# Hybrid decoder layer on one core: the last layer norm placed behind the first up weights, a ring shared by U and the down-weight sums, and row tiles used as the up projection's wide tiles

## The chip, the cores and the metric

The kernel runs on one core of one Trainium2 chip. The metric is the device time of one execution in microseconds, lower is better. All inputs and the output are float32.

## The reference, cut to what matters

One layer is computed on 2048 tokens of width 1024, with 16 learned tokens put ahead of them. An input projection feeds three mixers (a short convolution, a gated linear recurrence and a pooling group), whose outputs go through one output projection. Then:

```python
x = layer_norm(ALPHA * x + mix, ln1_g, ln1_b)
u = causal_dwconv(x @ w_up, w_ffn_conv, b_ffn_conv)     # w_up: 1024 x 5632, three taps over tokens
gate, val = jnp.split(u, 2, axis=-1)
ffn = (jax.nn.silu(gate) * val) @ w_down                # w_down: 2816 x 1024
out = layer_norm(ALPHA * x + ffn, ln2_g, ln2_b)
```

## The kernel before, in words

**Precision.** Each float32 operand is split into a high part (ScalarE cast, line 109) and a low part (VectorE difference, line 110), and each product is three TensorE matmuls: high by high, high by low, low by high.

**Mixers** (class Mixers, 0 to about 956 us). The tokens go in four blocks of 512 (b = 0 to 3). `out_proj` (lines 583 to 603) multiplies by w_o in two halves of columns, adds the residual to row tiles of 128 x 1024 (line 596), normalizes the rows (`layer_norm`, `norm_rows`, lines 188 to 208: bn_stats 199, square root on ScalarE 202, two fused VectorE passes 205 and 207) and stores them to x1 in DRAM (line 603). Of the last block this is done by `run_last`. `columns` (line 643) later reads x1, transposes it on TensorE (line 667) and writes x1T. Row tiles come from the pool `rows`, a ring of six.

**Up projection** (class Ffn, about 956 to 1940 us). x @ w_up is computed in two halves of 1024 tokens (b = 0, 1) by a Winograd form of Strassen's scheme: of the four blocks of x and of w_up, sums are made, and seven products stand for eight. A pair (`up_pair`, lines 895 to 963) is one tile of 128 gate columns and one of 128 value columns; there are 22 pairs per half. Its products, in this order, are a11 x b11, s2 x t2, a12 x b21, s1 x t1, s3 x t3, s4 x b22, a22 x t4 (`product`, line 892): 7 x 4 x 3 matmuls, 168 in half 0 (two column groups each) and 84 in half 1. ScalarE copies the first result to a tile U (line 921), and VectorE adds the others onto U, cg and cv (926, 935, 940, 944, 948). cg and cv also take two halo columns from GpSimd (905, 906). Then come the convolution (956, 959), silu (961) and the product yv (962). Before the change U, cg, cv and yg have one tile each and yv three. Every two pairs (ya and yb) give four sums on GpSimd into a tile a_t (975 to 978) and seven stores to a_ops (982); there is one tile a_t, used by `prepare` and `fetch` too.

- Weights: `load_pair` (829) loads them; in half 0 the weight sums s1 to s4 are made on GpSimd (846 to 849) and stored to s_up (852, 853), in half 1 they are loaded back (841, 842). `weights` (871) splits them. For the very first pair `begin` (864) loads and splits early: a11 and a12 lie in two row tiles.
- x operands: `prepare(0)` makes those of half 0. `prepare(1)` (740) makes those of half 1 on the side, in four steps: four piece loads from x1T (737), four GpSimd sums (751 to 754) into a_t, seven stores to x_ops (760). `fetch` and `take` (763 to 795) read all seven operands back during the last pair of half 0 and split them into the place of the old ones, each once its product has been done: first operand into a_t, the others through the ring `piece` of four tiles of 128 x 512.
- Down-weight sums: `down_sums` (987 to 1005) runs on the side of half 1 in 44 steps, each with two loads (996) into a piece, four GpSimd instructions (1000 to 1003) and one store (1004).

**Down projection** (`down`, from about 1940 us): seven products again, layer norm, output.

**What orders the work.** TensorE runs in program order. On every other engine and DMA queue a scheduler at build time fixes the order: among the instructions whose inputs and buffer slots are free by its own reckoning it takes the one earliest in the program. `high_priority(offset=AHEAD)` moves weights 1000 instructions ahead, and `layer_norm` is moved 300 back (BEHIND). Slots of a ring are given out as they come free. `weave` (1091) places two steps of the side work after each pair. On the chip each queue then runs strictly in its order. Loads and stores of the up stage go through SyncE's queue (SP).

## Time and profile before

| | us |
|---|---|
| median of 3 runs | 2404.72 (2399.98 to 2404.72) |
| profiled execution | 2401.31 |
| its span | 2399.6 |
| TensorE busy | 2262.4 (94%) |
| VectorE busy | 1678.5 (70%) |
| ScalarE busy | 890.0 (37%) |
| GpSimd busy | 852.0 (36%) |

Engines in the profile: PE is TensorE's matmuls, PEld its weight loads, DVE is VectorE, ACT ScalarE, POOL GpSimd, SP SyncE, and SPq, ACTq, POOLq are their queues. Times in rows are us from the span's start and durations in us, unless a row is a summary with "min/median/max" or "mean ns". "[x <-Y]" means that the engine sat idle for x us before the instruction and that Y ended the wait. PEclk is the granted TensorE clock as a share of full speed. An "xN" counts instructions.

### The profile page before, as it was taken

Reading aid. Unit: us, or ns where it says so; the run is one execution under the profiler, and the core shown is the slowest. Engines: PE = TensorE matmul, PEld = TensorE weight load, DVE = VectorE, ACT = ScalarE, POOL = GpSimd, SP = SyncE. Lnnn points to the kernel's source line nnn. Section 1 sums busy time; section 2 is a strip of 40 time slices with the busy share of each in tenths; the row PEclk is TensorE's granted clock in tenths of the full one; section 3 lists DMA queues with packets and bytes.
Section 4 is the critical chain, followed back from the end, with each engine's and each line's share of the span. In section 5 each row is a group of like instructions: output and inputs, shape, how many; then the busy total and the mean of one; then the engine's idle time right before and its main releaser. Section 6 shows DMA issues by size and latency. Waiting matters only on the chain.

```text
span 2399.6 us, 34046 instructions
## 1 busy us (share of the span) xinstructions
PE 2262.4 (94%) x12692; PEld 1930.7 (80%) x12692; DVE 1678.5 (70%) x2277; ACT 890.0 (37%) x1400; POOL 852.0 (36%) x870
## 2 busy tenths in 40 slices
PE   8999999999999998899979998877899999999996
PEld 6898777788888886799979997666788887887785
DVE  4676868687867878777767788655677766476658
ACT  3234322422342244344423445323344454334332
POOL 3451523152423344344465445677311113000300
PEclk9999999999999999899989999988999999999998
DMA  5212223322632264455675447677544476567553
GB/s 205 71 63 98 71 71 117 126 79 80 200 121 80 79 196 167 159 192 176 221 237 185 152 155 230 197 210 212 178 140 146 141 259 226 185 207 274 179 192 132
DMA packets 183737, 384.36 MB, mean 160 GB/s; under 512 B 17026, under 2 KB 78674, under 8 KB 183444
## 3 DMA queue, kind: packets, MB, share of 16 engines
q1 hardware_dynamic: 168180, 339.81, 43.0%
q10 hardware_dynamic: 14496, 40.06, 4.6%
q0 software_dynamic: 896, 2.33, 0.4%
q8 instruction: 99, 1.62, 0.3%
q14 instruction: 66, 0.54, 0.1%
HBM read 274.58 MB, written 107.55 MB: 159 GB/s over the span
## 4 chain that ended last, share of the span: by engine, by line
PE 69%; POOL 8%; DVE 8%; DMA 6%; issue 6%; ACT 2%; SPq 1%; POOLq 0%; DVEq 0%; ACTq 0%
PE bank L892 25%; PE bank L1035 13%; PE bank L114 9%; PE bank L116 8%; PE bank L115 8%; PE bank L397 3%; DVE w_lo L110 3%; DMA piece<-in_w_down_dram 1%; DMA row<-x 1%; POOL piece L1001 1%; POOL piece L1002 1%; POOL piece L1000 1%; DVE row L205 1%; DVE row L207 1%; DMA piece<-x_ops 1%
## 5 line engine op out<-in xcount | busy, mean ns | idle before, releaser
L110 DVE TENSOR_TENSOR w_lo<-raw,w_hi 128x512 fp32r<-128x512 f32 (+1 forms) x467 | 481.5, 1048 | 288.2 <-ACT w_hi L109 278.3
L109 ACT CAST w_hi<-raw 128x512 fp32r<-128x512 f32 (+1 forms) x467 | 359.3, 787 | 785.6 <-PE bank L116 261.2
L1035 PE MATMUL bank<-w_hi,w_lo 128*128 128x512 f32 x616 | 241.9, 393 | 10.2 <-DVE w_lo L110 10.2
L1035 PE MATMUL bank<-w_hi 128*128 128x512 f32 x616 | 240.4, 390 | 3.6 <-ACT w_hi L109 3.6
L1035 PE MATMUL bank<-w_lo,w_hi 128*128 128x512 f32 x616 | 240.4, 390 | 0.0
L114 PE MATMUL bank<-xhi,w_hi 128*128 128x512 f32 (+1 forms) x640 | 234.3, 366 | 0.0
L109 ACT CAST w_hi<-s 128x1024 fp32r<-128x1024 f32 x88 | 92.1, 1048 | 379.6 <-PE bank L892 248.3
L110 DVE TENSOR_TENSOR w_lo<-s,w_hi 128x1024 fp32r<-128x1024 f32 x88 | 125.8, 1430 | 144.2 <-ACT w_hi L109 144.2
L116 PE MATMUL bank<-xhi,w_lo 128*128 128x512 f32 (+1 forms) x640 | 225.1, 352 | 0.1
L115 PE MATMUL bank<-xlo,w_hi 128*128 128x512 f32 (+1 forms) x640 | 224.4, 351 | 0.0
L1035 PEld LDWEIGHTS bank<-w_hi,w_lo 128*128 128x128 f32 x616 | 116.0, 188 | 39.6 <-DVE w_lo L110 16.0
L1035 PEld LDWEIGHTS bank<-w_hi 128*128 128x128 f32 x616 | 116.0, 188 | 27.7 <-ACT w_hi L109 4.1
L1035 PEld LDWEIGHTS bank<-w_lo,w_hi 128*128 128x128 f32 x616 | 115.9, 188 | 25.1
L1068 POOL TENSOR_TENSOR row<-row,du 128x512 f32<-128x512 f32 x24 | 47.6, 2015 | 248.3 <-DVE du L1066 246.5
L116 PEld LDWEIGHTS bank<-xhi,w_lo 128*128 128x128 f32 x640 | 120.2, 188 | 17.3 <-DVE w_lo L110 0.5
L114 PEld LDWEIGHTS bank<-xhi,w_hi 128*128 128x128 f32 x640 | 120.5, 188 | 16.4 <-ACT chi L109 0.5
L115 PEld LDWEIGHTS bank<-xlo,w_hi 128*128 128x128 f32 x640 | 120.7, 189 | 15.0 <-issue 0.7
L959 DVE SCALAR_TENSOR_TENSOR yv<-cv,f_taps,yv 128x1024 f32<-128x1024 f32 x88 | 120.9, 1374 | 9.8 <-POOL cv L906 3.1
L892 PE MATMUL bank<-xb22h,w_hi 128*128 128x258 f32 (+2 forms) x264 | 77.5, 348 | 50.1 <-DVE cv L935 50.1
L959 DVE SCALAR_TENSOR_TENSOR yg<-cg,f_taps,yg 128x1024 f32<-128x1024 f32 x88 | 120.2, 1366 | 2.9 <-POOL cg L905 1.0
L114 PE MATMUL bank<-w_hi,xhi 128*128 128x512 f32 x272 | 112.9, 415 | 7.8 <-ACT xhi L109 7.8
L423 POOL TENSOR_TENSOR work<-work,pre 128x256 f32<-128x256 f32 (+1 forms) x96 | 89.0, 927 | 83.7 <-DVE pre L426 60.8
(291 smaller groups left out, 5766.0 us busy)
## 6 DMA issues: line engine op xcount, KB each, us to landing
raw<-a_ops SPq DMA_DIRECT2D x70, 512.0 KB, 4.7
raw<-in_w_up_dram SPq DMA_DIRECT2D x66, 512.0 KB, 4.6
raw<-in_w_feat_dram SPq DMA_DIRECT2D x64, 512.0 KB, 3.3
s_up<-s SPq DMA_DIRECT2D x44, 512.0 KB, 2.7
a_ops<-a_t SPq DMA_DIRECT2D x88, 256.0 KB, 2.0
s<-s_up SPq DMA_DIRECT2D x44, 512.0 KB, 4.6
raw<-s_down SPq DMA_DIRECT2D x40, 512.0 KB, 3.6
a_ops<-yv SPq DMA_DIRECT2D x66, 256.0 KB, 2.4
```

The costliest lines, as they stand in the source:

```text
L109: self.nc.scalar.copy(hi, src)
L110: self.nc.vector.tensor_sub(lo, src, hi.bitcast(F32))
L114: mm(out, lhsT=a_hi, rhs=b_hi, start=first, stop=False)
L115: mm(out, lhsT=a_hi, rhs=b_lo, start=False, stop=False)
L116: mm(out, lhsT=a_lo, rhs=b_hi, start=False, stop=last)
L205: nc.vector.scalar_tensor_tensor(r[:n], in0=r[:n], scalar=mv[:n, t, 0:1], in1=self.g_sb[:n], op0=ALU.subtract, op1=ALU.mult)
L397: mm(pt[:, t * P:(t + 1) * P], lhsT=ka[:, c:c + P], rhs=qa[:, c:c + P], start=True, stop=True)
L423: self.key_eng.tensor_mul(postv[:, :, 0, :], postv[:, :, 0, :], prev[:, :, 1, w - 1:w].to_broadcast(end))
L892: mm(u[:, 0:n], lhsT=wp[:, kc], rhs=xp[o][k][:, at:at + n], start=start, stop=k == 3 and i == 2, skip_group_check=True)
L959: nc.vector.scalar_tensor_tensor(y, in0=c[:, d:UT + d], scalar=self.taps[:, i, d:d + 1], in1=y, op0=ALU.mult, op1=ALU.add)
L1035: mm(bank, lhsT=x, rhs=y, start=first and k == 0 and i == 0, stop=k == HK - 1 and i == 2, skip_group_check=True)
L1068: nc.gpsimd.tensor_add(rows[t][:, f], rows[t][:, f], us[u])
```

## The change

The pool `rows` is opened on the other side of memory and stays open through the up projection; cg, cv, yg and yv of every pair are taken from its six tiles. The layer norm and the x1 stores of the last block of tokens become `end_block`, called after the split of the first pair's weights instead of at the end of `out_proj`; gain and shift are loaded a second time for it, into the tile a_t. `prepare(1)` stores only the four sums, with one DMA per step, and `fetch` reads b11, b21 and b22 from x1T. `take` becomes a generator: four of its seven operands are taken during the last pair of half 0 (after the first three products and at the end) and three during the first pair of half 1. In half 1, U is a tile of the ring `piece` (four tiles, now 514 wide), which the down-weight sums use at that time. The stores of the up weight sums are written into the program at the start of their own pair instead of the next one. The constants of the up stage are released together with it.

```diff
 def open_out(self, ctx):
...
-        self.rows = ctx.enter_context(self.tc.tile_pool(name="rows", bufs=6, side="right"))
...
+    def open_rows(self, ctx):
+        self.rows = ctx.enter_context(self.tc.tile_pool(name="rows", bufs=6, reuse_waits="tile"))
...
-    def load_norm(self, pool, g, b):
-        self.g_sb = pool.tile([P, D], F32, tag="ln_g", name="ln_g")
+    def norm_tiles(self, pool):
+        return [pool.tile([P, D], F32, tag=f"ln_{i}", name=f"ln_{i}") for i in "gb"]
+    def load_norm(self, tiles, g, b):
+        self.g_sb, self.b_sb = tiles
...
 def out_proj(self, b, half, res):
...
-        if half == 1:
-            cm.layer_norm(res[:TT], P)
...
+        if half == 1 and b + 1 < NB:
+            self.end_block(b, res)
+
+    def end_block(self, b, res):
+        cm, nc, tiles = self.cm, self.nc, self.row_tiles(b)
+        cm.layer_norm(res[:TT], P)
+        if b == 0:
+            cm.layer_norm(res[TT:], NM)
+        for (c, n), r in zip(tiles, res):
+            (nc.scalar if b + 1 < NB else nc.sync).dma_start(self.x1[b * TB + c:b * TB + c + n, :], r[0:n])
...
 class Ffn, __init__:
-        self.x_dram = [None] + [dpool.tile([7, P, 4 * UT // 2], F32, name=f"x_ops{b}") for b in range(1, UB)]
+        self.x_dram = [None] + [dpool.tile([4, P, 4 * UT // 2], F32, name=f"x_sums{b}") for b in range(1, UB)]
...
 def prepare(self, b):
...
+                if b:
+                    nc.sync.dma_start(self.x_dram[b][:, :, k * w:(k + 1) * w].rearrange("i p c -> p i c"), t)
+                    continue
...
-                for i, o in enumerate(X_OPS):
-                    if b == 0:
-                        cm.split(self.x_hi[o][k][:, at:at + w], self.x_lo[o][k][:, at:at + w], ops[o])
-                    else:
-                        nc.sync.dma_start(self.x_dram[b][i, :, k * w:(k + 1) * w], ops[o])
+                for o in X_OPS:
+                    cm.split(self.x_hi[o][k][:, at:at + w], self.x_lo[o][k][:, at:at + w], ops[o])
...
 def fetch(self, b):
...
+        def source(o, k):
+            if o[0] == "t":
+                return self.x_dram[b][int(o[1]) - 1, :, k * h:(k + 1) * h]
+            c = 2 + b * UT + (int(o[2]) - 1) * h
+            return self.cm.x1T[(int(o[1]) - 1) * 4 + k, :, c:c + h]
...
+        whole = self.a_tile()
+        for o in X_OPS:
             for k in range(4):
-                raw = self.piece()
-                self.nc.sync.dma_start(raw, self.x_dram[b][i, :, k * h:(k + 1) * h])
+                raw = whole[:, k, :] if o == X_OPS[0] else self.piece()
+                self.nc.sync.dma_start(raw, source(o, k))
                 yield o, k, raw
...
 def take(self, b):
...
-        def done(o):
+        while ready:
             for _ in range(4):
...
+            yield
...
-    def y_tile(self, name):
-        return self.ypool.tile([P, UT + 2], F32, tag="yv", name=name, bufs=3)
...
-    def piece(self):
-        return self.ypool.tile([P, UT // 2], F32, tag="piece", name="piece", bufs=4)
+    def piece(self, name="piece", n=UT // 2):
+        return self.ypool.tile([P, XW], F32, tag="piece", name=name, bufs=4)[:, 0:n]
...
 def load_pair(self, b, j):
...
-        self.store_sums()
-        self.store_sums = lambda: None
...
+    def store_sums(self, j, sums):
+        for i, s in enumerate(sums):
+            self.nc.sync.dma_start(self.s_up[j, :, i * 1024:(i + 1) * 1024], s)
...
 def up_pair(self, b, j, begun=None, done=lambda: None):
...
-        w = self.weights(*(begun or self.load_pair(b, j)))
-        U = self.upool.tile([P, XW], F32, tag="u", name="u", bufs=1)
-        cg = self.upool.tile([P, UT + 2], F32, tag="cg", name="cg", bufs=1)
-        cv = self.upool.tile([P, UT + 2], F32, tag="cv", name="cv", bufs=1)
+        w, sums = begun or self.weights(*self.load_pair(b, j))
+        if not b:
+            self.store_sums(j, sums)
+        U = self.piece("u", XW) if b + 1 == UB else self.upool.tile([P, XW], F32, tag="u", name="u", bufs=1)
+        cg, cv = (cm.wide_row()[:, 0:UT + 2] for _ in range(2))
...
-        done("b11")
+        done()
...
-        done("t1")
...
-        yg = self.upool.tile([P, UT], F32, tag="yg", name="yg", bufs=1)
-        yv = self.y_tile("yv")[:, 0:UT]
+        yg, yv = (cm.wide_row()[:, 0:UT] for _ in range(2))
...
         nc.vector.tensor_mul(yv, yg, yv)
+        done()
         return yv
...
 def up(self, b, begun=None):
...
+            if j == 0:
+                ya = self.up_pair(b, j, begun, lambda: next(taking, None))
+            else:
+                ya = self.up_pair(b, j)
             yield
...
+            if j + 1 == HK and b + 1 < UB:
+                taking = self.taking = self.take(b + 1)
+                yb = self.up_pair(b, j + HK, None, lambda: next(taking))
...
 hybrid_layer_kernel:
             xctx = ExitStack()
+            cm.open_rows(xctx)
...
-                ffn = Ffn(ctx, cm, dpool, x1, w_up, w_ffn_conv, b_ffn_conv, w_down, out[0])
+                ffn = Ffn(xctx, cm, dpool, x1, w_up, w_ffn_conv, b_ffn_conv, w_down, out[0])
...
-                drive(mix.run_last(), pending)
+                last_rows = []
+                drive(mix.run_last(last_rows), pending)
             ffn.open_weights(wctx)
             with xctx:
                 ffn.open_up(xctx)
+                begun = ffn.weights(*begun)
+                norm = ffn.a_tile().rearrange("p i c -> p (i c)")
+                cm.load_norm((norm[:, 0:D], norm[:, D:]), ln1_g, ln1_b)
+                mix.end_block(NB - 1, last_rows)
```

## Rows read from the trace of the kernel before

**Rows 1.** The page's head: span and number of instructions.

```profile
span 2399.6 us, 34046 instructions
```

**Rows 2.** Windows, line 892: us, PE busy (x), PEld busy (x), PEclk, DMA share, GB/s.

```profile
1475.80:1709.30 233.50, 190.50 (x758) 151.20 (x757) 0.90 0.68 205
1740.00:1934.00 194.00, 194.00 (x840) 157.27 (x839) 1.00 0.42 140
955.90:990.70 34.80, 23.44 (x168) 23.01 (x169) 0.80 0.37 137
...
1199.00:1283.00 84.00, 66.77 (x523) 65.88 (x523) 0.90 0.69 232
...
1447.90:1475.80 27.90, 22.73 (x89) 16.88 (x89) 0.94 0.74 241
```

**Rows 3.** Chain that ended last, one undisturbed pair of half 0.

```profile
1013.59 20.32 PE bank L892 x168
```

**Rows 4.** TensorE's waits from 940 to 1940 us, in total, times, longest.

```profile
PE bank L892 <- DVE cv L935: 50.1, 9, 14.5
PE bank L892 <- ACT u L921: 14.8, 6, 6.4
PE bank L892 <- DVE w_lo L110: 7.2, 1, 7.2
PE bank L892 <- ACT w_hi L109: 4.1, 1, 4.1
```

**Rows 5.** Timeline at the first pair: ScalarE, then VectorE, then GpSimd.

```profile
961.87 0.30 ACT L202 ACTIVATE ln_rs<-ln_mv,eps 128x4 f32<-128x4 f32 x1 [13.30 <-DVE ln_mv L200]
962.07 1.98 ACT L109 CAST w_hi<-s 128x1024 fp32r<-128x1024 f32 x2
...
970.26 2.35 DVE L110 TENSOR_TENSOR w_lo<-s,w_hi 128x1024 fp32r<-128x1024 f32 x2
...
971.56 2.19 POOL L846 TENSOR_TENSOR s<-raw 128x512 f32<-128x512 f32 x1 [35.19 <-DVE w_lo L110]
```

**Rows 6.** Groups of instructions on VectorE from 940 to 971 us.

```profile
L199 DVE BATCH_NORM_STATS2 ln_st<-row 128x6 f32<-128x512 f32 x8 | 5.2, 666 | 0.0
```

**Rows 7.** Line 207 in the whole span: duration min, median, max in ns.

```profile
L207 DVE SCALAR_TENSOR_TENSOR row<-row,ln_rs,ln_b x33: 1253/1279/2319, 397.1 to 2394.8; 128x1024 f32<-128x1024 f32 x32, 16x1024 f32<-16x1024 f32 x1
```

**Rows 8.** Window 1000 to 1200 us, all engines (PE, PEld, DVE, ACT, POOL).

```profile
1000.00:1200.00 200.00, 200.00 (x1663) 200.00 (x1662) 143.58 (x179) 87.07 (x120) 89.35 (x78) 1.00 0.55 193
```

**Rows 9.** Preparing half 1: line 760 in all, then SyncE and GpSimd timelines.

```profile
L760 SPq DMA_DIRECT2D x_ops<-piece x12: 319/379/637, 1189.9 to 1244.1; - x12
...
1240.38 4.04 SPq L760 DMA_DIRECT2D x_ops<-piece  x3
1244.48 0.43 SPq L852 DMA_DIRECT2D s_up<-s  x1
...
1248.59 1.26 POOL L847 TENSOR_TENSOR s<-s,raw 128x512 f32<-128x512 f32 x1 [6.30 <-DMA s_up<-s]
```

**Rows 10.** Tile piece from 1426 to 1476 us: ns, first and last start.

```profile
L790 ACT CAST xb21h<-piece x4: 619/621/623, 1440.6 to 1446.6; 128x512 fp32r<-128x512 f32 x4
...
L790 ACT CAST xb22h<-piece x4: 617/620/622, 1461.6 to 1464.7; 128x512 fp32r<-128x512 f32 x4
```

**Rows 11.** Down sums: line 1003 between seven halo copies; line 1000; first and last start; landings.

```profile
1507.50:1678.30 170.80, 21.38 (x36) 0.89 0.69 205
...
L1000 POOL TENSOR_TENSOR piece<-piece 128x128 f32<-128x128 f32 x44 | 29.5, 671 | 49.6 <-DMA piece<-in_w_down_dram 49.6
...
L996 SPq DMA_DIRECT2D piece<-in_w_down_dram x88: 368/492/1614, 1478.2 to 1679.4; - x88
...
L1004 SPq DMA_DIRECT2D s_down<-piece x44: 359/367/930, 1487.1 to 1693.7; - x44
...
s_down<-piece SPq DMA_DIRECT2D x44, 256.0 KB, 2.8
piece<-in_w_down_dram SPq DMA_DIRECT2D x86, 128.0 KB, 4.3
```

More of the change, by code (lines that the diff above doesn't have):

```diff
@@ L180, in take_columns @@
             yield
-    def load_norm(self, pool, g, b):
-        self.g_sb = pool.tile([P, D], F32, tag="ln_g", name="ln_g")
+    def norm_tiles(self, pool):
+        return [pool.tile([P, D], F32, tag=f"ln_{i}", name=f"ln_{i}") for i in "gb"]
+    def load_norm(self, tiles, g, b):
+        self.g_sb, self.b_sb = tiles
         self.nc.gpsimd.dma_start(self.g_sb, bcast_rows(g, P))
-        self.b_sb = pool.tile([P, D], F32, tag="ln_b", name="ln_b")
         self.nc.gpsimd.dma_start(self.b_sb, bcast_rows(b, P))
@@ L597, in out_proj @@
                                            op0=ALU.mult, op1=ALU.add)
-        if half == 1:
-            cm.layer_norm(res[:TT], P)
-            if b == 0:
-                cm.layer_norm(res[TT:], NM)
-            for (c, n), r in zip(tiles, res):
-                (nc.scalar if b + 1 < NB else nc.sync).dma_start(self.x1[b * TB + c:b * TB + c + n, :], r[0:n])
+        if half == 1 and b + 1 < NB:
[7 more added lines that the diff above has]
+            (nc.scalar if b + 1 < NB else nc.sync).dma_start(self.x1[b * TB + c:b * TB + c + n, :], r[0:n])
     def run(self, pending):
@@ L636, in pool_and_conv, with run_last @@
             self.pool_maps()
[L638 to L639 removed]
+    def run_last(self, res):
         for half in range(2):
@@ L766, in fetch @@
         h = UT // 2
-        for i, o in enumerate(X_OPS):
-            if i == 0:
-                whole = self.a_tile()
-                self.nc.sync.dma_start(whole, self.x_dram[b][i].rearrange("p (k c) -> p k c", k=4))
-                yield from ((o, k, whole[:, k, :]) for k in range(4))
-                continue
+        def source(o, k):
[5 more added lines that the diff above has]
+        for o in X_OPS:
             for k in range(4):
-                raw = self.piece()
-                self.nc.sync.dma_start(raw, self.x_dram[b][i, :, k * h:(k + 1) * h])
+                raw = whole[:, k, :] if o == X_OPS[0] else self.piece()
+                self.nc.sync.dma_start(raw, source(o, k))
                 yield o, k, raw
@@ L783, in take @@
         ready = deque(next(loads) for _ in range(8))
-        def done(o):
+        while ready:
             for _ in range(4):
-                o_, k, raw = ready.popleft()
-                assert o_ == o
+                o, k, raw = ready.popleft()
                 hi, lo = self.x_hi[o][k][:, 0:w], self.x_lo[o][k][:, 0:w]
@@ L849, in load_pair @@
                 nc.gpsimd.tensor_sub(sa[:, h:], wa[:, h:], sa[:, 0:h])
-                def store():
-                    nc.sync.dma_start(self.s_up[j, :, 0:2 * h], sa)
-                    nc.sync.dma_start(self.s_up[j, :, 2 * h:], sb)
-                self.store_sums = store
         return wa, wv, sa, sb
+    def store_sums(self, j, sums):
+        for i, s in enumerate(sums):
+            self.nc.sync.dma_start(self.s_up[j, :, i * 1024:(i + 1) * 1024], s)
     def split_a22(self, wv):
@@ L880, in weights @@
         ops = {"a11": (a1, 0), "a12": (a1, 1), "s2": (s24, 0), "s4": (s24, 1), "s3": (s31, 0), "s1": (s31, 1)}
-        return {o: (p[0][:, half[i]], p[1][:, half[i]]) for o, (p, i) in ops.items()} | {"a22": a22}
+        return {o: (p[0][:, half[i]], p[1][:, half[i]]) for o, (p, i) in ops.items()} | {"a22": a22}, (sa, sb)
     def product(self, banks, w, o, groups, first):
@@ L930, in up_pair @@
             nc.scalar.copy(cg[:, c1], u[:, 0:n])
-        done("b21")
+        done()
         A = banks()
@@ L944, in up_pair @@
             nc.vector.tensor_add(cg[:, c2], U_[:, s:], u[:, s:n])
-        done("b22")
         self.product(B, w["a22"], "t4", groups, False)
@@ L962, in up_pair @@
         nc.vector.tensor_mul(yv, yg, yv)
+        done()
         return yv
@@ L968, in up @@
         h = UT // 2
+        taking = self.taking
         for j in range(HK):
-            ya = self.up_pair(b, j, begun if j == 0 else None)
+            if j == 0:
+                ya = self.up_pair(b, j, begun, lambda: next(taking, None))
+            else:
+                ya = self.up_pair(b, j)
             yield
-            done = self.take(b + 1) if j + 1 == HK and b + 1 < UB else (lambda o: None)
-            yb = self.up_pair(b, j + HK, None, done)
+            if j + 1 == HK and b + 1 < UB:
+                taking = self.taking = self.take(b + 1)
+                yb = self.up_pair(b, j + HK, None, lambda: next(taking))
+            else:
+                yb = self.up_pair(b, j + HK)
             t = self.a_tile()
```

15 lines of the change are left out of this document (4 added, 11 removed).

## The prediction

> **What bounds the kernel now.** I read the page first: span 2399.6 us, profiled execution 2401.3 us, 1.7 us around the span [rows 1]. The median of the three runs, 2404.7, lies 3.4 above it and all three within 0.2%; the sums below start from 2401.3. About 0.2%, some 5 us, is what a measurement of this kernel can tell from no change.
>
> TensorE is the engine that should never stop, so I looked at windows of its up products (line 892) [rows 2] and at what it waits for there [rows 4]. An undisturbed pair takes 20.3 us in half 0 [rows 3] and, ten pairs in 194.0 us, 19.4 us in half 1. Against that, four stretches lose time. The first pair takes 34.8 us: **14.5 lost**. 523 matmuls (3.11 pairs, 63.2 us) take 84.0 us while the operands of half 1 are prepared: **20.8 lost**. The first pair of half 1 takes 27.9 (89 matmuls, five of them its neighbours'): **8.5 lost**. The nine pairs after it take 233.5 us where 9 x 19.4 = 174.6 would do: **59 lost**, while the 44 down-weight sums run; behind them nothing is lost. Together 103 us, 4.3% of the span. Nearly all of it shows as TensorE waiting for DVE's write of cv or for ScalarE's copy to U [rows 4]: both are symptoms, so each stretch needs its own chain.
>
> **Part A, layer norm behind the weights.** ScalarE stands 13.3 us before the norm's square root (line 202), and the casts of the first pair's weight sums sit behind it in its queue; DVE's matching differences come right after the last norm instruction [rows 5]. TensorE waits 4.1 + 7.2 us for them [rows 4]; the rest of the 14.5 is matmuls at a mean granted clock of 0.80 in that window, between the two levels of 1.2 and 2.4 GHz, after idle time [rows 2]. With the weights cast first, that chain goes. What moves is 8 bn_stats (5.2 us), 4 + 4 fused passes (10.2 at the median of line 207) and about 1 us of small ones, 16 us of DVE [rows 6, 7], plus four x1 stores on SP and a second load of gain and shift on POOL, which stood idle 35.2 us there [rows 5], so those two loads cost nothing; were POOL busy they would cost their own transfer. DVE is busy 143.6 of 200 us in the pairs that follow [rows 8], so a pair has 20.3 x 0.28 = 5.7 us free and 16 us need three pairs. In them every late DVE write holds TensorE. The SP stores now wait for a later norm with the next weight loads queued behind them. Also, the residual rows now hold four of the six slots from which cg, cv, yg and yv must come, and the first pair's a11 operand the other two; those two come free after its third product, in time for cg and cv. Ends: nothing gained (the rows must be stored before yg can start) to 16 gained; I take 3 us of new waiting, nearer to the free end because yg is first written after the sixth product, some 17 us into the pair, and the norm's 16 us can start at once: **-11.5**.
>
> The Trainium skill (SBUF — State Buffer, Who interferes with whom) says a DVE instruction with two SBUF inputs and a GpSimd instruction reading SBUF exclude each other. Line 207 spans 1.25 to 2.32 us [rows 7], which agrees; by it the 8 passes, now beside POOL's weight sums, could cost up to 8 us more.
>
> **Part B, preparing half 1.** 28 stores become 4: the 12 stores of raw pieces [rows 9] and the 4 x 4 separate sum stores go, and later reads of b11, b21, b22 come from x1T, as many bytes as before. In the worst pair SP stands in piece stores until 1244.5, each waiting for its load; the store of the weight sums is issued behind them, POOL's next weight sum waits 6.3 us for that store, and casts, differences and cv follow [rows 9]; TensorE's wait there is the 14.5 us longest of its cv waits [rows 4]. Without the piece stores that queue is open. Late next is the merged store: it waits for all four sums and holds the single a_t tile until 1 MB has landed, and the up sums need the same tile. Ends: 0 to 20.8; I keep 7 us of waiting, nearer to the clean end because the blocking instructions themselves are removed: **-14**.
>
> **Part C, the turn.** Seven operands pass through four pieces, one operand per 7 us or so: casts start at 1440.6 for b21 and 1461.6 for b22, three operands on [rows 10]. Spreading the takes over two pairs changes only their priority, not this round. But U of half 1 now needs one of the four pieces. Loads of t3 and b22 stand ahead of it in program order, so U gets the first piece freed by b22, about 1462.5. On the clock of before, the third product needs U two products (2 x 19.4 / 7 = 5.5 us) after the pair's start at 1447.9 [rows 2], at 1453.4: 9 us of waiting, in exchange for the 8.5 that this pair loses now, part of it for t4, which TensorE then reaches later. Ends: -8.5 (U gets a slot at once, the takes spread well) to +10 (one operand's round more); I take **+2**.
>
> **Part D, U in the ring of the down sums.** POOL's order holds 36 sums between seven halo copies, six per pair [rows 11], so 44 sums are spread over 7.3 pairs, 142 us of TensorE. On the chip they take 216 us, 4.9 us each, 19.6 us for one round of a piece: loads landing after 4.3, four POOL instructions, a store landing after 2.8, and queueing in between; POOL alone waits 49.6 us for their loads [rows 11]. Halo copies and weight loads stand behind them in POOL's and SP's queues. 216 - 142 = 74 us of lag, 59 of it paid by TensorE. With U holding a piece from its first copy (after 2.8 us) to its last use at the pair's end, 0.86 of a pair, the sums have 3.14 pieces: 6 x 3.14 / 4 = 4.7 per pair, 9.4 pairs, 182 us. If the round stays 19.6 us, they take 44 x 19.6 / 3.14 = 275 us: 93 of lag, of which little is covered, since U itself now waits for a sum's store only 3 us before TensorE needs it: 90 paid, **31 worse**. If the round shrinks to 14 us, the transfers and POOL's work with little queueing, they take 196: 14 of lag, 3 covered, **48 better**. I take 16.5 us, one fewer sum queueing ahead on POOL: 231 us, 49 of lag, 5 covered, 44 paid: **-15**.
>
> cg and cv in a ring of six instead of one tile each, yg and yv likewise: at most ya, yb, cg', cv', yg', yv' live together, six, so nothing waits in steady state; if a_ops stores are late, the next cg waits as it does now. The weight sums' two stores per pair stand earlier in the program, b11 is fetched in four DMAs instead of one: at 0.4 us of SP per issue [rows 9] hidden by SP's free time, and if that were gone worth the 6.3 us wait of part B at a time. Rows on the other side of memory, constants closed earlier: no instruction, nothing. Down stage and mixers are untouched.
>
> **Sum.** -11.5 - 14 + 2 - 15 = -38.5: 2401.3 - 38.5 = **2363**.
>
> **Rivals.** (1) *The ring throttles fully*: the sums slow to the pace at which POOL and SP serve them and the lag vanishes. For: behind them not one microsecond is lost [rows 2]. Against: three pieces in one round still run ahead of the program. D becomes -56, 3 us of the 59 staying: 2322. (2) *U waits for sums* (slower side): at each pair's third product ScalarE stands in order before U's copy until a sum's store has landed, with the weight casts behind it. It decides when the round stays above 18 us: 44 x 18 / 3.14 = 252, 70 of lag, more than is paid now. For: the round's parts are mostly latency and queueing [rows 11], which one fewer piece shortens little. Against: POOL waits 49.6 us for loads [rows 11], time in which it could catch up. D is +31 and C +10: 2401.3 - 11.5 - 14 + 10 + 31 = 2417. The Trainium skill (Perfetto Trace Analysis, Optimization Strategy) speaks for this one: a gap that repeats can mean too little memory for the next tile. The trace shows such a gap, 50.1 us in nine cv waits [rows 4], though not whether the piece ring causes it. (3) *The norm doesn't get out of the way*: the row ring binds, A is 0, and TensorE waits for norms and stores as before: 2374.
>
> **Chances.** Forecast 0.45; (1) 0.18; (2) 0.22; (3) 0.10; 0.05 for losses not named, such as a reordered down start. The forecast itself, with B and A at their worse ends, reaches 2389; with A and C at their better ends it reaches 2348. Holding (1) at 2322 and the centre of (2) at 2417 gives 2318 to 2420. Slower is (2), 0.22, less what of it lies near 2401 and more from the unnamed; within 0.2% 0.09 from between forecast and (2); faster 0.69.
>
> **What would show it.** Right: no wait for a weight difference in the first pair, norms spread between DVE's up writes; no piece stores on SP and no 14 us gap before 1260; five rather than six sums per pair, running to about pair ten of half 1, and waits per pair of about 4 us. Wrong: U's copy as the longest wait in half 1 (rival 2); sums still six per pair, which would mean that U costs them no slot; first pair still near 35 us (rival 3); nine pairs near 175 us (rival 1).

## The result, and the profile after

The changed kernel takes 2332.24 us (median; 2329.08 to 2332.45) against 2402.35 us for the kernel before on the same chip: a ratio of 0.9706, 95% interval 0.9682 to 0.973. One further execution of it took 2364.72 us and is left out of the comparison; it was not profiled, so whether its cause is the one found for long executions of e4 and e7 at the end of the experiments is not shown. The direction and the range of the prediction hold, its value of 2363 lies 31 us too high.

The head of the page after (two lines of its section of slices: TensorE's busy share and its granted clock, in tenths; the dip in the middle is the turn):

```profile
span 2330.7 us, 33935 instructions
## 1 busy us (share of the span) xinstructions
PE 2249.5 (97%) x12692; PEld 1923.7 (83%) x12692; DVE 1673.3 (72%) x2277; ACT 890.6 (38%) x1400; POOL 860.0 (37%) x872
PE   8999999999999999999998997999999999999996
...
PEclk9999999999999999999999998999999999999998
```

The span is 68.9 us shorter. I split it at the starts of TensorE's pairs. These are the after windows of its up products (columns as in [rows 2]): the first pair, the stretch that prepares half 1 (four whole pairs here), the first pair of half 1, the nine pairs behind it.

```profile
956.10:982.10 26.00, 23.59 (x168) 23.05 (x168) 0.87 0.46 163
1192.20:1284.70 92.50, 83.99 (x675) 82.97 (x674) 0.98 0.64 218
1428.60:1463.90 35.30, 22.32 (x86) 17.42 (x85) 0.81 0.67 209
1463.90:1639.00 175.10, 175.10 (x757) 141.90 (x757) 1.00 0.60 192
```

The fourth line is the change: 233.5 us have become 175.1, at full clock, and TensorE does not stop once. The third line is what it cost: the turn went from 27.6 to 35.3 us. TensorE's waits of the up stage, 940 to 1900 us, answer to [rows 4]:

```profile
PE bank L895 <- ACT u L926: 12.9, 3, 11.0
PE bank L895 <- DVE row L940: 12.2, 6, 3.8
PE bank L118 <- DVE w_lo L113: 1.2, 1, 1.2
```

Some 50 us of waiting for cv have become 12, and 11.0 of the 12.9 for U are one wait, at the turn. Stage by stage, between starts of pairs, with every kernel run (us, of the profiled execution; "4 pairs" are pairs 12 to 15 of half 0, "last" its 22nd; "9 pairs" and "11 pairs" lie behind the first of half 1; an undisturbed pair is 20.3 us in half 0 and 19.45 in half 1). The profiled executions of e4 and e7 took 2375.0 and 2375.7 us, so their pairs of half 1 do not go with the medians beside them:

```
                    first  2nd  4 pairs  last | first  9 pairs  11 pairs   median
before               34.8  22.6  102.3   21.8 | 27.6   233.5    213.9    2402.35
after                26.0  21.1   92.5   22.0 | 35.3   175.1    214.0    2332.24
e1_u_own             25.8  21.1   95.0   22.0 | 38.6   221.6    214.0    2383.80
e2_before_ring       34.2  24.6  100.4   21.8 | 27.7   188.4    235.4    2381.08
e3_hold_piece        26.7  21.1   92.3   22.1 | 38.1   216.5    214.0    2379.56
e4_old_gain          34.9  22.4   93.5   22.0 | 35.0   182.4    238.2    2344.59
e5_norm_first        25.7  21.1   95.4   23.9 | 34.5   175.1    214.0    2339.57
e6_u_first           25.9  21.1   94.3   22.0 | 37.7   175.0    214.0    2337.27
e7_old_stores        25.8  21.1  102.2   21.7 | 34.4   187.5    231.0    2359.97
e8_takes_last        25.7  21.2   94.1   22.0 | 26.8   186.8    235.0    2356.64
e9_takes_ring        26.3  21.1   94.0   22.0 | 38.5   175.1    214.0    2335.70
e14_six              25.8  21.1   95.1   26.6 | 30.3   175.7    214.0    2331.83
e15_takes_ring_six   25.8  21.1   94.9   24.6 | 27.6   175.1    213.9    2329.38
e16_a_sums_dve       25.8  21.1   93.6   22.0 | 26.9   175.1    214.0    2328.78
```

From before to after: first two pairs -10.3, preparation -9.8, turn +7.9 with its last pair, nine pairs -58.4; the rest of the span +1.7. Nine of these kernels prepare half 1 in the same way (after, e1, e3 to e6, e8, e9, e16) and take 92.3 to 95.4 us for the four pairs: after lies at the low end, and differences of some 3 us there cannot be told from none.

### The profile page after: what moved, and what is told of

Read it like the earlier page. It is cut to its first block, busy times and chain, and to the rows that moved or that the text cites. A ratio compares the mean times of both kernels' runs of the same rounds, so it can differ in the third digit from the quotient of the medians.

```text
span 2330.7 us, 33935 instructions
## 1 busy us (share of the span) xinstructions
PE 2249.5 (97%) x12692; PEld 1923.7 (83%) x12692; DVE 1673.3 (72%) x2277; ACT 890.6 (38%) x1400; POOL 860.0 (37%) x872
## 4 chain that ended last, share of the span: by engine, by line
PE 80%; DVE 7%; POOL 4%; DMA 4%; issue 3%; ACT 1%; SPq 0%; DVEq 0%; ACTq 0%; POOLq 0%
PE bank L895 32%; PE bank L1044 14%; PE bank L117 9%; PE bank L118 9%; PE bank L119 9%; PE bank L402 3%; DVE w_lo L113 2%; POOL pw L563 1%; ACT w_hi L112 1%; DMA row<-x 1%; DVE row L210 1%; PE bank L415 1%; PE bank L676 1%; DVE row L959 1%; PE bank L485 1%
## 5 line engine op out<-in xcount | busy, mean ns | idle before, releaser
L959 DVE SCALAR_TENSOR_TENSOR row<-row,f_taps 128x1024 f32<-128x1024 f32 x176 | 237.0, 1348 | 9.6 <-ACT row L956 4.5
L956 ACT ACTIVATE row<-row,f_bias,f_taps 128x1024 f32<-128x1024 f32 x88 | 109.6, 1246 | 78.7 <-DVE row L950 74.9
L117 PE MATMUL bank<-w_hi,chi 128*128 128x512 f32 x272 | 112.1, 412 | 2.8 <-ACT w_hi L112 2.8
```

Source lines behind the costliest of these rows:

```text
L117: mm(out, lhsT=a_hi, rhs=b_hi, start=first, stop=False)
L956: nc.scalar.activation(y, c[:, 2:UT + 2], AF.Identity, bias=self.bias[:, i:i + 1], scale=self.taps[:, i, 2:3])
L959: nc.vector.scalar_tensor_tensor(y, in0=c[:, d:UT + d], scalar=self.taps[:, i, d:d + 1], in1=y, op0=ALU.mult, op1=ALU.add)
```

## The experiments

### What freed the nine pairs

The order of the queues shows it first. Before, GpSimd had six sums, on average, between the halo copies of two pairs [rows 11]. After, all along half 1, it has exactly two. Two pairs of GpSimd after (of the four instructions of a sum only the first is shown, those of the a tile are left out; 910 and 911 are the halo copies for cg and cv):

```profile
1705.72 0.46 POOL L1009 TENSOR_TENSOR piece<-piece 128x128 f32<-128x128 f32 x1 [8.77 <-DMA piece<-in_w_down_dram]
...
1708.82 0.46 POOL L1009 TENSOR_TENSOR piece<-piece 128x128 f32<-128x128 f32 x1
...
1712.10 0.18 POOL L910 COPY row<-f_halo 128x2 f32<-128x2 f32 x1
1720.23 0.18 POOL L911 COPY row<-f_halo 128x2 f32<-128x2 f32 x1 [7.95 <-ACT row L956]
1724.13 0.81 POOL L1009 TENSOR_TENSOR piece<-piece 128x128 f32<-128x128 f32 x1 [3.71 <-DMA piece<-in_w_down_dram]
...
1726.51 1.45 POOL L1009 TENSOR_TENSOR piece<-piece 128x128 f32<-128x128 f32 x1
...
1734.27 0.19 POOL L910 COPY row<-f_halo 128x2 f32<-128x2 f32 x1
```

The sentence on rings ahead of the prediction, that slots are given out as they come free, is wrong: a ring hands its tiles out in the order of the program. The program has two sums, a U, two sums, a U; with U in the ring, no sum of the next pair can be moved ahead of this pair's U. The runs below show it: GpSimd has two sums per pair, from the fourth pair of half 1 on at the latest, in every kernel with U in the ring, and five to eight until they are done in the three without (before, e1, e3).

**e1_u_own** takes U out of the ring again:

```diff
-        U = self.piece("u", XW) if b + 1 == UB else self.upool.tile([P, XW], F32, tag="u", name="u", bufs=1)
+        U = self.upool.tile([P, XW], F32, tag="u", name="u", bufs=1)
```

> The changed kernel, but U has a tile of its own in half 1 too. Theory 1 (the ring hands its tiles out in program order, so that one U per pair lets only two down-weight sums through per pair): without U in the ring the sums run ahead again, about six per pair, and the nine pairs behind the first of half 1 take about 233 us as before instead of 175 us; the first pair loses its 11 us wait for U and gets some 3 us of waiting for t4 back. Sum: 2332 + 58 - 8 = about 2382 us. Theory 2 (the row ring of six for cg, cv, yg and yv is what took the cv waits away): the nine pairs stay at 175 us and the time falls to about 2324 us.

Measured: 2383.80 us, ratio 0.9927 (0.9911 to 0.9944). The nine pairs lose 46.5 us again (221.6 - 175.1). The total came out as expected, its parts did not: the nine pairs take 221.6 us for 233, and the first pair of half 1, expected to get 8 us shorter, got longer, 38.6 us for 35.3. Why it did is told under the turn.

**e2_before_ring** puts U into the ring of the kernel before, from the second pair of half 1 on, and does nothing else:

```diff
-        U = self.upool.tile([P, XW], F32, tag="u", name="u", bufs=1)
+        U = self.piece() if b + 1 == UB and j else self.upool.tile([P, XW], F32, tag="u", name="u", bufs=1)
```

> The kernel before, with one edit: in half 1, from its second pair on, U is a tile of the ring of pieces. Theory 1: the sums are paced at two per pair and the 59 us lost in the nine pairs go, nothing else moves: 2402 - 58 = about 2344 us. Theory 2 (row ring): the cv waits stay, since cv still has a single tile, and the time stays above 2385 us.

Measured: 2381.08 us, ratio 0.9916 (0.9901 to 0.993). Both expectations miss. Two sums per pair, as expected, but the loss is spread instead of gone: 13.3 us in the nine pairs and 21.4 in the eleven behind. TensorE's waits from 1420 us on in this kernel, and below them what its GpSimd waits for (1463 to 1900):

```profile
PE bank L892 <- DVE cv L935: 25.1, 12, 5.5
```

```profile
POOL cv L906 <- DVE yv L959: 17.6, 9, 2.7
POOL cg L905 <- DVE yg L959: 13.6, 4, 7.4
```

With a single cg and a single cv the halo copy must wait for the convolution of the pair before, and with it all that GpSimd does behind it. With row tiles it waits for a row of the ring, which is free earlier: where no sums are left (pairs 15 to 21 of half 1) the copy for cv ends 6.4 us after its pair's start in the kernel before, and 3.6 us or less in e1.

That this wait is what e2 lacks is not shown. e8, further down, has the row ring, takes U from the ring from the second pair on as e2 does, and loses nearly as much. Put in a row, the kernels differ step by step as follows (us from the start of half 1 to the start of its 22nd pair, the sums of three columns above):

```
before                                                         475.0
e2      U in the ring from the second pair on                  451.5   -23.5
e8      the change at all other places (the row ring too),
        but all operands taken in the last pair of half 0      448.6    -2.9
e9      U in the ring in the first pair too                    427.6   -21.0
after   the operands taken in two pairs                        424.4    -3.2
```

So it is U's place in the ring that brings nearly all, in two steps, and the second of them is the subject of the section on e8. The step that adds the row ring, with the change's other parts, brings 2.9 us. The 11.9 us that the nine pairs of e1 save against before are no measure of it either: e1's first pair is 11.0 us longer, and its first sum starts 1.9 us ahead of the nine pairs instead of 8.2 us behind their start. No run has single tiles and U in the ring in every pair, so whether the 175.1 us need the row ring stays open.

**e3_hold_piece** tells order from number: U has its own tile, and one of the four pieces is held by a dummy through half 1.

```diff
...
+            if b + 1 == UB and j == 0:
+                hold = self.piece("hold")
+                nc.gpsimd.memset(hold[:, 0:1], 0.0)
+            if b + 1 == UB and j + 1 == HK:
+                nc.gpsimd.tensor_add(hold[:, 0:1], yb[:, 0:1], hold[:, 0:1])
```

> The changed kernel with U in a tile of its own, and one of the four pieces held by a dummy from the end of the second pair of half 1 to its last pair: the sums have three pieces but nothing paces them. Theory 1 (order, not number): the sums still run ahead at five to six per pair and the pairs beside them lose 40 to 90 us; 2365 to 2410 us. Theory of the prediction (the number of pieces decides; 3 pieces, a shorter round of 14 to 16.5 us): the loss is between 14 and 49 us; 2338 to 2373 us. Theory 2 (row ring): no loss, about 2324 us.

Measured: 2379.56 us, ratio 0.9912 (0.9896 to 0.9928); 5.5 sums per pair in GpSimd's order, 41.4 us lost in the nine pairs. Three pieces instead of four bring 5 us (221.6 - 216.5), U's place in the order the other 41.

### What freed the first pair and the preparation

**e4_old_gain** drops the second copy of gain and shift: the late norm uses the first one.

```diff
-                norm = ffn.a_tile().rearrange("p i c -> p (i c)")
-                cm.load_norm((norm[:, 0:D], norm[:, D:]), ln1_g, ln1_b)
```

> The changed kernel, but the layer norm of the last rows uses the gain and shift that were loaded at the start, whose memory the up weights take over, instead of a second copy. It is still built behind the first weights. Theory 1 (the weights wait for whoever last read their memory; the second copy is what frees them): the first pair goes back from 26.0 us towards the 34.8 us of before, the pair behind it from 21.1 to about 22.6, and the total from 2332.2 to about 2342. Theory 2 (the order in which the program issues the steps is enough): the first pair stays at 26 us, the total within 2 us of 2332.

**e5_norm_first** keeps the copy and writes the norm ahead of the weights:

```diff
-                begun = ffn.weights(*begun)
...
                 mix.end_block(NB - 1, last_rows)
+                begun = ffn.weights(*begun)
```

> The changed kernel with its second copy of gain and shift, but the layer norm of the last rows is issued before the first up weights, as in the kernel before. Theory 1 (memory held the weights back): the first pair stays near 26 us, the total within 2 us of 2332. Theory 2 (program order on ScalarE and VectorE held them back): the first pair goes back to about 35 us, the total to about 2342.

Measured: the first pair takes 34.9 us in e4 and 25.7 in e5; medians 2344.59 (0.9727 to 0.9855) and 2339.57 (0.9708 to 0.983), each with one execution far above its others (2375.0 and 2363.2). Theory 1 holds for the first pair in both. e5's total lies over its range (2330 to 2334): the preparation takes 95.4 us and the last pair of half 0 23.9, and why the last pair does stays unexplained. ScalarE's square root, after and in e4 (the second has the wait of [rows 5] again, 13.30 us):

```profile
953.34 2.00 ACT L112 CAST w_hi<-s 128x1024 fp32r<-128x1024 f32 x2 [4.68 <-PE bank L118]
...
971.66 0.30 ACT L207 ACTIVATE ln_rs<-ln_mv,eps 128x4 f32<-128x4 f32 x1 [4.32 <-DVE ln_mv L205]
```

```profile
962.74 0.30 ACT L207 ACTIVATE ln_rs<-ln_mv,eps 128x4 f32<-128x4 f32 x1 [13.30 <-DVE ln_mv L205]
962.95 1.98 ACT L112 CAST w_hi<-s 128x1024 fp32r<-128x1024 f32 x2
```

It is not the place of the norm in the program that lets the weights go first but the second copy: without it the weights are scheduled behind the norm wherever the norm is written. That the tiles of the weights lie on the memory of the first copy is read from the code, not measured.

**e7_old_stores** brings back the seven stores per step and the fetch from them:

```diff
-                if b:
-                    nc.sync.dma_start(self.x_dram[b][:, :, k * w:(k + 1) * w].rearrange("i p c -> p i c"), t)
-                    continue
...
+                    else:
+                        nc.sync.dma_start(self.x_dram[b][i, :, k * w:(k + 1) * w], ops[o])
...
```

> The changed kernel with the stores of the kernel before in the preparation of half 1: seven stores for each of four steps and all seven operands fetched from there, instead of one store of the four sums and three operands fetched from the transposed rows. Theory 1 (the 24 stores less are what the four pairs beside the preparation gained): pairs 11 to 14 go from 92.5 us back to about 102, the total to about 2342. Rival (rows of the ring for the wide tiles did it, the stores are covered): they stay at 92 to 95 us, the total within 3 us of 2332.

Measured: the four pairs take 102.2 us, before 102.3, after 92.5. TensorE's longest wait from 1190 to 1290 us is the 14.5 us of [rows 4] again, then after for comparison:

```profile
PE bank L892 <- DVE row L937: 14.5, 1, 14.5
```

```profile
PE bank L895 <- DVE row L940: 6.6, 2, 3.8
```

So the stores were it, and the row ring does nothing there. The total of this kernel says less, for a reason that follows below: its executions took 2341.5, 2344.5, 2375.4 and 2375.7 us.

### The turn

After, ScalarE has U's copy behind the first cast of b22 (its timeline), and TensorE waits for it (its timeline):

```profile
1442.46 0.62 ACT L800 CAST xb22h<-piece 128x512 fp32r<-128x512 f32 x1 [1.36 <-DMA piece<-x1T]
1444.69 0.59 ACT L926 COPY u<-bank 128x512 f32<-128x512 f32 x1 [1.61 <-DVE xb22l L802]
```

```profile
1445.33 0.80 PE L895 MATMUL bank<-xb21h,w_hi 128*128 128x512 f32 x1 [11.01 <-ACT u L926]
```

That is the chain of part C: U gets a piece that b22 has left.

**e6_u_first** gives U its own tile in the first pair of half 1 only:

```diff
-        U = self.piece("u", XW) if b + 1 == UB else self.upool.tile([P, XW], F32, tag="u", name="u", bufs=1)
+        U = self.piece("u", XW) if b + 1 == UB and j else self.upool.tile([P, XW], F32, tag="u", name="u", bufs=1)
```

> The changed kernel, but in the first pair of half 1 U has its own tile; from the second pair on it is a piece. Theory 1: the 11 us wait for U goes, t4 is then waited for by about 3 us, the pacing stays: 2332 - 8 = about 2324 us. Rival (the round of the seven operands through four pieces sets the turn anyway): TensorE waits for t3, b22 or t4 instead, and the gain is 0 to 2 us: 2330 to 2332 us.

Measured: 2337.27 us, ratio 0.9731 (0.9717 to 0.9746), 5 us over the change. U's wait is gone (0.8), and TensorE waits for operands instead; its waits from 1415 to 1470 us:

```profile
PE bank L895 <- POOL xt3l L802: 4.7, 1, 4.7
PE bank L895 <- ACT xt4h L800: 2.6, 1, 2.6
PE bank L895 <- DVE xt4l L802: 2.0, 1, 2.0
```

The pair takes 37.7 us, and both expectations miss: the wait was a symptom here. The operands' round through four pieces sets the turn, and with U on its own, spreading the takes over two pairs has lengthened it (e8, next, has 26.8).

**e8_takes_last** takes all seven operands in the last pair of half 0, as before, with U as in e6. **e9_takes_ring** does the same with U in the ring.

```diff
 def up_pair (behind each of the last four products):
+        done()
...
-        done()
         return yv
 def up:
-                ya = self.up_pair(b, j, begun, lambda: next(taking, None))
+                ya = self.up_pair(b, j, begun)
...
-                yb = self.up_pair(b, j + HK, None, lambda: next(taking))
+                yb = self.up_pair(b, j + HK, None, lambda: next(taking, None))
```

> The changed kernel, but all seven operands of half 1 are taken in the last pair of half 0 as in the kernel before, and U has a tile of its own in the first pair of half 1. Theory 1 (spreading the takes over two pairs, and U queued behind them, is what the turn lost): the first pair of half 1 goes from 35.4 us back to 27.6 us, the total to about 2324.5, below both kernels. Rival (the turn is set by something else, the ring's four pieces or the down weights): the pair stays at 35 us or over, or the last pair of half 0 grows by what the next one gains, and the total stays within 3 us of 2332.

> The changed kernel with all seven operands taken in the last pair of half 0, U still in the ring in every pair of half 1. Theory 1 (U is queued behind the pieces of the last operands, and with all of them ahead of it, it waits longer): the first pair of half 1 takes 38 to 45 us, the total 2334 to 2342. Rival (the place of the takes alone sets the turn, U's queue is covered): 28 to 30 us, about 2326.

Measured: e9 2335.70 us (ratio 0.9702 to 0.9747), first pair 38.5, U's wait 16.7: theory 1. So each of the two edits at the turn by itself costs it some 11 us (26.8 to 37.7 for the spread takes, 26.8 to 38.5 for U in the ring), and both together 8.5 (35.3): their waits cover for each other. In e8 the turn does what was expected, 26.8 us, and the total does not: 2356.64 us (0.9795 to 0.9842). The pairs behind it take 421.8 us where after takes 389.1. I had not thought of that; it needs a theory of its own.

### Why e8 lost its gain again

In half 1, SyncE and GpSimd go round once per pair: loads of two sums, the sums, the a tile, its stores, the weights' loads, the halo copies. The end of the halo copy for cv, counted from the start of its pair, marks where this round stands (worked out from the traces, pairs 2 to 14 of half 1):

```
after        7.0  4.5  2.6  3.6  2.6  3.6  1.7  3.6  1.1  3.6 -0.4  3.6 -0.4
e2           6.9  6.7  9.3  7.7  8.7  7.9  9.3 10.4  8.8  7.6  8.7  8.9  8.7
e4           7.0  4.7  4.8  4.7  7.5  8.9  7.0  6.4  9.3 10.4  7.0  5.8  9.3
e7           8.7  4.9  7.2  6.4  9.2 10.8  4.0  4.7  4.7  4.9  8.7  9.3  7.1
e8           2.9  6.7 10.9 10.3  4.2  4.9  6.9  5.9  8.8  9.3  7.2  5.4  7.0
e15         -0.4  3.6 -2.1  3.6 -1.8  3.6 -2.2  3.6 -0.5  3.6 -2.0  3.6 -2.1
e16          2.9  5.2  0.9  3.6 -4.7  3.6 -4.7  3.6 -4.7  3.6 -4.7  3.6 -4.7
```

Where nothing is lost the mark settles at 3.6 us and below, and GpSimd stands waiting for a row (the 7.95 us above): it has time left. The kernels that lose in half 1 (e2, the profiled executions of e4 and e7, e8) stand at 4 to 11 (e8 from the third pair on), and their waits of 2 us and more fall, but for one, in pairs at 8.9 and more. How it reaches TensorE, in the fifth pair of e8 (timelines of SyncE, ScalarE, VectorE, TensorE, lines between left out):

```profile
1527.62 0.33 SPq L994 DMA_DIRECT2D a_ops<-a_t  x1
...
1528.49 0.56 SPq L845 DMA_DIRECT2D s<-s_up  x1
```

```profile
1533.88 1.04 ACT L112 CAST w_hi<-s 128x1024 fp32r<-128x1024 f32 x1 [10.83 <-DMA s<-s_up]
```

```profile
1534.95 1.23 DVE L113 TENSOR_TENSOR w_lo<-s,w_hi 128x1024 fp32r<-128x1024 f32 x1 [8.52 <-ACT w_hi L112]
1536.10 0.68 DVE L940 TENSOR_TENSOR row<-u,bank 128x512 f32<-128x512 f32 x1
```

```profile
1536.83 0.80 PE L895 MATMUL bank<-xb22h,w_hi 128*128 128x512 f32 x1 [5.20 <-DVE row L940]
```

SyncE holds the weights' load behind the store of the a tile, which waits for GpSimd; ScalarE's cast waits for the load, VectorE's write of cv stands in its queue behind the difference of that cast, TensorE waits for cv. In e8 GpSimd has no sum ahead of the second pair's halo copy and four ahead of the third's, where after has two and two; e2 has the order of e8. GpSimd's work also takes longer in such a round: four of its groups from 1500 to 1900 us, after, and then in e4 (its execution of 2375 us); its other additions and subtractions differ in the same direction:

```profile
L1010 POOL TENSOR_TENSOR piece<-piece 128x128 f32<-128x128 f32 x38 | 21.5, 565 | 3.0
L1012 POOL TENSOR_TENSOR piece<-piece 128x128 f32<-128x128 f32 x38 | 19.3, 507 | 3.0
L986 POOL TENSOR_TENSOR a_t<-row 128x512 f32<-128x512 f32 x11 | 19.3, 1753 | 0.0
L984 POOL TENSOR_TENSOR a_t<-row 128x512 f32<-128x512 f32 x10 | 14.0, 1400 | 0.0
```

```profile
L1012 POOL TENSOR_TENSOR piece<-piece 128x128 f32<-128x128 f32 x38 | 32.4, 854 | 3.0
L1010 POOL TENSOR_TENSOR piece<-piece 128x128 f32<-128x128 f32 x38 | 29.2, 769 | 3.0
L986 POOL TENSOR_TENSOR a_t<-row 128x512 f32<-128x512 f32 x10 | 21.2, 2119 | 0.0
L984 POOL TENSOR_TENSOR a_t<-row 128x512 f32<-128x512 f32 x9 | 18.5, 2055 | 0.0
```

Three runs test it. **e14_six** is the changed kernel with six pieces in the ring, **e15_takes_ring_six** is e9 with six:

```diff
-        return self.ypool.tile([P, XW], F32, tag="piece", name=name, bufs=4)[:, 0:n]
+        return self.ypool.tile([P, XW], F32, tag="piece", name=name, bufs=6)[:, 0:n]
```

> The changed kernel with six pieces in the ring instead of four, nothing else. Theory 1 (number of pieces sets the turn, order sets the pairs): U no longer waits 11 us, the first pair of half 1 takes 28 to 31 us instead of 35.4, the nine pairs behind it stay at 175 us, the total about 2326. Theory 2 (the wait at the turn gives the sums' round its lead): the first pair is shorter by as much, but the pairs behind it take 185 us or more, the total 2332 or over.

> The changed kernel with all seven operands taken in the last pair of half 0 and six pieces in the ring instead of four; U stays in the ring in every pair of half 1. With six, the first U reuses a piece that was emptied early, so it has nothing to wait for, and the loads of the first two sums are issued right behind the operands. Theory 1 (the turn costs 8 us through the ring, and the pairs behind it stay at 19.45 us as long as the loads of the sums are issued early enough): the first pair of half 1 takes about 27 us, the nine pairs behind it 175 us, the total about 2324, below both kernels. Theory 2 (the wait at the turn is what gives the sums' round of SyncE and GpSimd its lead over TensorE; without it the round of about 20 us is on the path): the first pair takes 27 us but the nine pairs 185 to 205 us, the total 2340 to 2357.

Measured: e14 2331.83 us (0.97 to 0.9733): the turn falls to 30.3, the pairs stay at 175.7, but the last pair of half 0 rises by 4.6. e15 2329.38 us (0.9688 to 0.9721): turn 27.6, pairs 175.1, last pair +2.6. The pairs behind the turn follow theory 1 in both: the wait at the turn is not needed to keep the round on time, if a sum or two stand ahead of the second pair's halo copy (one in e14, two in e15, none in e8 and e2). That order alone does not ensure it, for e4 and e7 have it too. Both totals miss theirs, for the totals gain less than the turn does; in e15's profiled execution the start, the preparation and the last pair are longer than after's by 1.1, 2.4 and 2.6 us.

**e16_a_sums_dve** is e8 with less work in the round:

```diff
-            nc.gpsimd.tensor_sub(t[:, 1, :], ya[:, h:], ya[:, 0:h])
+            eng = nc.vector if b + 1 == UB else nc.gpsimd
+            eng.tensor_sub(t[:, 1, :], ya[:, h:], ya[:, 0:h])
...
```

> The kernel with all takes in the last pair of half 0 and U on its own in the first pair of half 1 (2356 us, with its pairs of half 1 at 20.7 to 21.3 us), and the four subtractions of each a tile in half 1 on VectorE instead of GpSimd; nothing else. Theory 1 (in that kernel the round of SyncE and GpSimd, loads of two sums, the sums, the a tile, the stores, has lost its lead over TensorE and is on the path): taking 4 us of GpSimd's work per pair out of the round gives the lead back, the 21 pairs behind the first go from 422 us back to about 389, the total to about 2324, below both kernels. Rival (something else slows those pairs: the weights' loads, VectorE or the transfers): the pairs stay at 415 us or more, the total at 2350 or over; with VectorE as the bound it rises further.

Measured: 2328.78 us (2323.69 to 2335.55), ratio 0.9704 (0.9688 to 0.9719). The pairs are back at 389.1 with the turn at 26.9. What GpSimd's halo copy of cv waited for from 1500 to 1850 us, in e8 (with its wait for the loads of the sums) and in e16 (the two longest):

```profile
POOL piece L1012 <- DMA piece<-in_w_down_dram: 142.1, 16, 10.2
POOL row L911 <- ACT row L960: 1.9, 1, 1.9
```

```profile
POOL row L911 <- DVE row L963: 78.9, 8, 10.6
POOL row L911 <- ACT row L960: 10.6, 1, 10.6
```

In e8 GpSimd comes to the copy too late to wait for it. It is not busy all the time, for it stands 142.1 us before the loads of the sums, which SyncE issues behind the stores that wait for GpSimd: it is the round of the two that has no time left. In e16 GpSimd stands 89.5 us before the copy, waiting for VectorE and ScalarE. So the round was the bound. e16 takes work out of it and also lets the stores of the a tile wait for VectorE instead of GpSimd; which of the two counts for more is not separated. That GpSimd's instructions take longer does not suffice for a loss: those of the sums average 678 to 895 ns in e16, as long as in e4, and nothing is lost.

The round is late in the executions of e4 and e7 near 2375 us too: the profiled execution of each is one, and its marks stay above 3.6 us up to the last pair. Why those executions fall behind and others of the same kernels do not stays open.

The profiled execution of e16 (2323.69) is 8.8 us below the changed kernel's, as the turn says; its median lies 3.5 below, that of e15 2.9, measured on other chips, and the three intervals of the ratio overlap. Neither is shown to beat the change.

## Why the prediction was right or wrong

- **Part A**, -11.5 predicted, -10.3 measured (first two pairs). The norm went to the gaps of VectorE as described, and the weight differences came early (the square root now follows them). The step that named the cause was too narrow: that the casts stand behind the square root in ScalarE's queue is so, but what put them there is gain and shift (e4, e5). I had booked their second load as a cost of nothing; it is the condition of the gain. So the number came out well for a reason that was not the one given: the new order in the program brings nothing without the copy (34.9 us in e4) and is not needed with it (25.7 in e5). The norm's four line-212 passes took 1.27 to 2.30 us and the four of line 210 1.23 to 1.55, together some 2.8 us over eight times 1.25: of the "up to 8 us more" worked out beside the Trainium skill (SBUF — State Buffer, Who interferes with whom), that much is there.
- **Part B**, -14 predicted, -9.8 measured, mechanism confirmed by e7. The term mis-sized is the 7 us of remaining waits: 92.5 us against 4 x 20.3 leaves 11.3, of which 8.5 are waits (6.6 for cv, 1.9 for U) and the rest longer matmuls (84.0 us busy for 81.2, granted clock 0.98).
- **Part C**, +2 predicted, +7.9 measured. U's wait came as forecast and where forecast, 11.0 us for 9. The step that failed is that this comes "in exchange for the 8.5 that this pair loses now": beside U's wait the pair still waits 2.0 us for cv, and its matmuls take 2.9 us longer than at full clock (22.3 us for 19.45, granted clock 0.81). That spreading the takes "changes only their priority, not this round" is wrong as well: with U on its own it costs the pair 10.9 us (e8 to e6), with U in the ring it saves 3.2 (e9 to after).
- **Part D**, -15 predicted, -58.4 measured: the step that failed. It treated the ring as a count, "6 x 3.14 / 4 = 4.7 per pair", and asked how long a round takes. The ring is an order: two sums per pair with U in it (after, e2), five to eight without (e1), and five to seven without and with one piece less (e3), so that with U in the ring sums never run ahead at all. Rival (1), at 0.18, has the outcome right (its sign, nine pairs near 175 us, is what came), though the sums are held by the order fixed at build time and not by the pace of the queues; its argument against ("three pieces in one round still run ahead of the program") was the same mistake. That the row ring was costed at nothing is not refuted: the step that adds it brings 2.9 us (e2 to e8), and whether the rest needs it was not run. What the forecast had no term for is the place of the very first sums, ahead of or behind the second pair's halo copies: 21.0 us between e8 and e9.
- Rival (2) rested on a wait for pieces and on the Trainium skill (Perfetto Trace Analysis, Optimization Strategy), by which a repeating gap can mean too little memory. The runs differ from it here: with fewer free tiles for the sums the gap closed. The gap came from side work that stood ahead of urgent work in the queues.
- Of the 30 us between sum and result, D makes -43, C +6, B +4, A and the rest +3. The forecast's own terms, at their better ends, reach 2348; that 2332 lies within 2318 to 2420 is owed to rival (1), held at 2322, and not to the working of D.

## What to carry to other kernels

A tile taken from a ring that side work uses is also a pacemaker: since this scheduler hands tiles out in program order, it keeps the scheduler from moving the side work ahead, and that can be worth more than the buffers it costs. Look at how many side steps stand between two urgent instructions in each queue, and at whether the side engine still has time left before the urgent one; when it has none, in-order queues pass its lateness on in every round, and a saving elsewhere (e8) is given back more than once. And when one compares kernels stage by stage, a stage's gain can be its neighbour's loss (e1: first pair +11.0, nine pairs -11.9), and two edits whose waits cover for each other cost less together than either alone (the turn: 10.9, 11.7, together 8.5).

## What the runs showed of the hardware that was not expected

GpSimd's subtractions last longer when its round falls in with VectorE's work differently: on average 1400 ns against 2055 for line 984 and 507 against 854 for line 1012, the same instructions in two executions (after and e4). The Trainium skill (SBUF — State Buffer, Who interferes with whom) says that a VectorE instruction with two SBUF inputs and a GpSimd instruction reading SBUF exclude each other. The two traces agree, instruction by instruction, for the 128x128 instructions of the sums from 1500 to 1900 us (worked out from their starts and ends). Of those that ran beside no VectorE instruction with two SBUF inputs, 184 in all, each took 451 to 469 ns, also where VectorE was reading a bank of TensorE's results. All 66 that took over 1000 ns, 19 after and 47 in e4, ran beside one with two SBUF inputs.
